# Each block of the normalised input h lies 64 bytes further on within 512 bytes than the block before it

## The chip, the cores and the metric

The kernel runs on one core of a Trainium2 chip. The metric is the device time of one execution in microseconds. Beside the times there is one profiled execution, whose trace names for each instruction its engine, its line in the kernel, its start and its duration.

## What is computed

The reference is one layer of a decoder trunk: an input of 512 positions by 1024 channels is normalised to h, h goes through one wide projection into 14,344 columns, and these feed two mixers (a chunkwise mLSTM and a differential attention), whose outputs are projected, gated, added and projected once more.

```python
h = rmsnorm(x, norm_g[l]) * (1.0 + scale[:, None]) + shift[:, None]
proj = h @ w_in[l]
(qm, km, vm, om, zm, im, fm, qa, ka, va, za, gm, ga) = jnp.split(proj, split_idx, axis=-1)
...
ym = hm @ w_proj_m[l]
...
ya = ha @ w_proj_a[l]
y = jax.nn.sigmoid(gm) * ym + jax.nn.sigmoid(ga) * ya
x = x + gate[:, None] * (y @ w_out[l])
return rmsnorm(x, final_g)
```

## The kernel before

All is float32. A product of two float32 matrices is made of three matmuls: each operand is split into a high part (`hi`, rounded to the matmul's format) and a low part (`lo`, what is left), and `mm3` (line 132) adds hi times hi, hi times lo and lo times hi into the same PSUM tile. One matmul takes 128 by 128 weights and streams up to 512 columns of the other operand, the moving one, past them. In the profile's rows the moving operand stands first behind the arrow: `acc<-h_hi,whi` is h moving over weights whi.

The normalised input lies transposed in two tiles, `h_hi` and `h_lo` (lines 338 and 339): 128 partitions, 8 blocks k of 128 channels each, 512 positions. A block is 2048 bytes of a partition. They are written block by block by ACT (line 614, high part) and DVE (line 616, low part) in the opening loop, and are read by nearly all the matmuls that follow:

- In the opening loop, block k is used in its own turn for the first columns of the attention (lines 622 to 629): six runs of three matmuls with h moving, and four with h as weights (`mm_v`).
- `proj_b` (line 342) is the projection into 128 columns, called 82 times for 656 runs: for k = 0 to 7 three matmuls of 512 columns, h moving over a weight tile (`whi`, `wlo`).
- `proj_w` (line 379) is the projection into the 512 value columns of an mLSTM head, with h as weights and the columns of `whi` and `wlo` moving: per weight tile, for four groups of positions, three matmuls with block 2q and three with block 2q + 1.
- `proj_v` (line 368), for the attention's values, is the same with 256 moving columns and twelve matmuls on a block.
- `if_gates` (line 519) has sixteen matmuls of h over one weight tile, two to a block.

`attn_proj` and `proj_m` have no h: the heads' outputs (`hh`, `hl`) move over `whi` and `wlo`. Two lines that make a sum over partitions, 509 and 510 (and 810 and 811, 837 and 838 in the mLSTM), have the constant tile `ones_r` as weights.

When the last projection of h is done, `out_weights` (line 865) reuses h's place: the output weights 0, 1 and 2 are split into blocks 0 and 1, 2 and 3, 4 and 5 of h_hi and h_lo, as 1024 elements in one piece. `out_mm` (line 974) has them moving, 512 or 256 columns at a time.

The constant tiles lie in a partition in the order in which they are named; each takes a multiple of 32 bytes. The two tiles `pad_before` and `pad_after` of 32 bytes each stand before h_hi and behind h_lo. With that, all blocks of h begin 32 bytes behind a multiple of 512. All tiles that the pools place behind them (the weights, the heads' outputs, q, k, v, the temporaries) are whole multiples of 512 bytes apart and begin at 288, that is 256 further on; the slices that the matmuls take begin at multiples of 512 bytes within them. `ones_r` lies ahead of h and begins at 224, 64 bytes before the place of the others.

TensorE takes its matmuls in the order in which the program issues them. While one matmul streams, the weights of the next are loaded.

Of the kernel before, what the change touches and what calls it, by code (L numbers as in the profile page):

```python
# [10 lines left out]
F32R = mybir.dt.float32r  # L11
# [3 lines left out]
S = 512  # L15
D = 1024
P = 128
NK = D // P
# [46 lines left out]
def hybrid_block_kernel(ctx: ExitStack, tc: tile.TileContext, xT, x, c, wada2, wada, win, wif, wpm, wpa, wout,  # L65
# [3 lines left out]
    const = ctx.enter_context(tc.tile_pool(name="const", bufs=1))  # L69
# [8 lines left out]
    def nm(s):  # L78
        _n[0] += 1
        return f"{s}_{_n[0]}"  # L80

    def tmp(w=512, dt=F32):
        return sb.tile([P, w], dt, tag="tmp", bufs=TB, name=nm("tmp"))

    def acc_ps():
        return acc.tile([P, 512], F32, tag="acc", name=nm("acc"))

    def core_ps():
        return core.tile([P, 512], F32, tag="core", name=nm("core"))
# [24 lines left out]
    def split(hi, lo, src, eng="act", scale=None):  # L114
        copy_r(eng, hi, src, scale)
        if scale is None:
            recent["dve"] = nc.vector.tensor_tensor(lo, src, hi.bitcast(F32), ALU.subtract)  # L117
        else:
            nc.vector.scalar_tensor_tensor(lo, src, scale, hi.bitcast(F32), ALU.mult, ALU.subtract)
# [5 lines left out]
    def inorder(inst):  # L125
        if last[0] is not None:
            tc.add_manual_dep(inst.ins, last[0].ins.name,
                              mybir.DependencyInfo(mybir.DependencyClass.NoSync, mybir.DependencyReason.DATA),
                              reason="issue order")
        last[0] = inst  # L130

    def mm3(ps, lhs, rhs, start, stop, head=False, swap=False):
        l, r = ((1, 0), (0, 1)) if swap else ((0, 1), (1, 0))
        a = nc.tensor.matmul(ps, lhs[0], rhs[0], start=start, stop=False)  # L134
        b = nc.tensor.matmul(ps, lhs[l[0]], rhs[l[1]], start=False, stop=False)  # L135
        c = nc.tensor.matmul(ps, lhs[r[0]], rhs[r[1]], start=False, stop=stop)  # L136
        last_mm[0] = c
        if head:
            inorder(a)
            inorder(b)  # L140
            inorder(c)

    def load_granule(src):
        raw = stg.tile([P, D], F32, tag="raw", name=nm("raw"))
        nc.sync.dma_start(raw, src)
        return raw
# [24 lines left out]
    for k in range(NK):  # L171
        t = sb.tile([P, S], F32, tag="hp", bufs=16, name=nm("xt"))
# [71 lines left out]
    for i in range(2):  # L244
        ps = core_ps()
        a = nc.tensor.matmul(ps, onesf[0:1, :], crow[:, i * S:(i + 1) * S], start=True, stop=True)
# [19 lines left out]
    for k in range(NK):  # L266
        i, start = (0, k == 0) if k < 5 else (1, k == 5)
        sq = xsum[i] if start else tmp()
        a = nc.scalar.activation(sq, xt[k], AF.Square, scale=1.0 / 32)
# [36 lines left out]
    ps = core_ps()  # L306
# [21 lines left out]
    for (a, b) in ((0, 512), (512, RL)):  # L328
        ps = core_ps()
# [5 lines left out]


    const.tile([P, 8], F32, name="pad_before")
    h_hi = const.tile([P, NK, S], F32R, name="h_hi")
    h_lo = const.tile([P, NK, S], F32R, name="h_lo")
    const.tile([P, 8], F32, name="pad_after")  # L340

    def proj_b(col, between=None):
        hi, lo = split_granule(win[GIDX[("B", col)]])
        ps = acc_ps()
        for k in range(NK):
            ksl = slice(k * P, (k + 1) * P)
            mm3(ps, (hi[:, ksl], lo[:, ksl]), (h_hi[:, k, :], h_lo[:, k, :]), k == 0, k == NK - 1)
            if k == 1 and between is not None:
                between()
        recent["pe"] = last_mm[0]  # L350
        return ps
# [68 lines left out]
    def evac_ka(ps):  # L420
        kh, kl = [], []
        for a, b in ((LO, HI), (HI, LO)):
            t, l = qk_tile(), qk_tile()
            nc.gpsimd.memset(l[b].bitcast(F32), 0.0)
            nc.scalar.copy(t[a], ps[a])
            nc.scalar.copy(t[b], ps[a])
            nc.vector.tensor_tensor(l[a], ps[a], t[a].bitcast(F32), ALU.subtract)  # L427
            kh.append(t)
            kl.append(l)
        return kh, kl  # L430
# [171 lines left out]
    for k in range(NK):  # L602
        raw = load_granule(win[GIDX[("F", k)]]) if k > 0 else first_raw
# [4 lines left out]
        a = nc.scalar.copy(hi, raw)  # L608
        issue_after(a, recent["act"])
        recent["act"] = a  # L610
        t, b = xt[k], mod[:, k:k + 1]
# [32 lines left out]
        if k == 4:  # L644
# [9 lines left out]
            a = nc.vector.tensor_scalar(agc, sm[:, SM_AG:SM_AG + 8], -0.5 / 256 * (1.0 - LAM_INIT), None, ALU.mult)  # L654
            mgc = const.tile([P, 16], F32, name="mgc")
            issue_after(a, h_dve)
            a = nc.vector.tensor_scalar(mgc, sm[:, SM_MG:SM_MG + 16], -0.25 / 4096, None, ALU.mult)
# [31 lines left out]
    for p in range(1, 4):  # L689
        for i in range(2):  # L690
# [3 lines left out]
            k = evac_ka(proj_b(C_KA + 128 * hd))  # L694
# [16 lines left out]
    ps = core_ps()  # L711
# [151 lines left out]
    wo = [None] * NK  # L863

    def out_weights(k):
        raw = stg.tile([P, D], F32, tag="raw", name=nm("raw"))
        nc.sync.dma_start(raw, wout[k])
        if k < 3:
            t = [x_[:, 2 * k:2 * k + 2, :].rearrange("p a b -> p (a b)") for x_ in (h_hi, h_lo)]
        elif k < 7:  # L870
            tag, bufs = {3: ("v", 2), 4: ("p", PB), 5: ("p", PB), 6: ("sw", 1)}[k]
            w2 = sb.tile([P, 2, D], F32R, tag=tag, bufs=bufs, name=nm("wo"))
            t = [w2[:, 0, :], w2[:, 1, :]]
        else:
            t = [stg.tile([P, D], F32R, tag=n_, name=nm(n_)) for n_ in ("whi", "wlo")]
        split(t[0], t[1], raw, eng="act")
        wo[k] = t
# [12 lines left out]
    for h in range(MH):  # L890
        q, k, v, hv = [], [], [], []
# [18 lines left out]
        for d in range(4):  # L910
            zv.append(silu2(proj_b(C_ZM + 512 * h + 128 * d)))
            tick()
            fill()
            if h == MH - 1:
                premerge(d, load_gate(d, tmp()))
                if d == 3:
                    out_weights(4)
        ssum = tmp()
        for d in range(4):
            ps = proj_b(C_OM + 512 * h + 128 * d)  # L920
            while len(hv) <= d:
                tick()
            t = tmp()
# [4 lines left out]
            else:  # L928
                t = tmp()
# [14 lines left out]
    for b in range(4, 8):  # L944
        ps = proj_b(C_GM + 128 * b, tick if b > 4 else None)
# [3 lines left out]
    for k in (3, 5, 6):  # L949
        out_weights(k)  # L950
# [4 lines left out]
    yt = []  # L955
# [12 lines left out]
    for k in (0, 1, 2, 7):  # L968
        out_weights(k)

    def rows(t):
        return slice(t * P, (t + 1) * P)

    def out_mm(ps, t, ns, ks):
        for k in ks:
            mm3(ps, (yt[k][0][:, rows(t)], yt[k][1][:, rows(t)]), (wo[k][0][:, ns], wo[k][1][:, ns]),
                k == 0, k == NK - 1)

    def residual(ps, xr, o, ns, ss):
# [8 lines left out]
    for n in range(2):  # L988
        out_mm(first[n], 0, halves[n], range(LATE))
    for t in range(NT):  # L990
        xr = stg.tile([P, D], F32, tag="raw", name=nm("xr"))
        nc.sync.dma_start(xr, x[rows(t), :])
        ss = sb.tile([P, 5], F32, tag="ss", bufs=2, name=nm("ss"))
        parts = halves if t < NT - 1 else (slice(0, 512), slice(512, 768), slice(768, D))
        os = [sb.tile([P, S], F32, tag="z", bufs=8, name=nm("o")) for _ in range(2)]
        for n, ns in enumerate(parts):
            ps = first[n] if t == 0 else acc_ps() if n % 2 == 0 else core_ps()
            ps = ps[:, 0:ns.stop - ns.start]
            out_mm(ps, t, ns, range(LATE if t == 0 else 0, NK))
            o = os[ns.start // 512][:, ns.start % 512:ns.start % 512 + ns.stop - ns.start]  # L1000
            residual(ps, xr, o, ns, ss[:, n:n + 1])
            if n < len(parts) - 1:
                nc.vector.tensor_add(ss[:, 3:4], ss[:, n:n + 1], epsc if n == 0 else ss[:, 3:4])
        n = len(parts) - 1
        nc.scalar.activation(ss[:, 4:5], ss[:, n:n + 1], AF.Sqrt, bias=ss[:, 3:4])
        nc.vector.reciprocal(ss[:, 4:5], ss[:, 4:5])
        for n, ns in enumerate(halves):
            if n == 0:
                nc.scalar.activation(os[n], xr[:, ns], AF.Copy, scale=ss[:, 4:5])
                nc.scalar.dma_start(out[rows(t), ns], os[n])  # L1010
            else:
                nc.vector.tensor_scalar(os[n], xr[:, ns], ss[:, 4:5], None, ALU.mult)
                nc.sync.dma_start(out[rows(t), ns], os[n])
# [70 lines left out]
```

## Time and profile before

| | us |
|---|---|
| median of 3 runs | 925.57 (925.35 to 926.0) |
| the profiled execution | 924.88 |
| its span, first to last instruction | 923.1 |
| TensorE, matmuls busy | 908.9 |
| VectorE (DVE) busy | 601.7 |
| ScalarE (ACT) busy | 454.9 |

The span is the part of the profiled execution's time that the trace covers. A busy time is the union of an engine's instructions. Matmuls overlap in the trace (each row lasts from its issue until its last result is through), so the pace of TensorE is the distance from one matmul's start to the next one's, which the timeline gives to 0.01 us, and not the duration in a row.

### The profile page before, as it was taken

How to read it: one execution, taken by the hardware profiler on the slowest of the kernel's cores; microseconds unless marked ns; L12 is line 12 of the kernel's file. 1: busy time of each engine (PE TensorE's matmuls, PEld its weight loads, DVE VectorE, ACT ScalarE, POOL GpSimd, SP SyncE). 2: the span in 40 equal slices, each digit the busy share in tenths (PEclk: the TensorE clock that was granted, in tenths of full speed). 3: DMA queues.
4: the chain of work that ended last, by engine and by line, in shares of the span. 5: the costliest groups of instructions: out<-in, count | busy, mean ns of one | idle time of the engine just before them, and what ended most of it. 6: DMA issues, size and time to landing. Idle time of an engine off the chain costs nothing.

```text
span 923.1 us, 11500 instructions
## 1 busy us (share of the span) xinstructions
PE 908.9 (98%) x4351; PEld 762.5 (83%) x4351; DVE 601.7 (65%) x975; ACT 454.9 (49%) x741; POOL 24.3 (3%) x56
## 2 busy tenths in 40 slices
PE   6999999999999999999999999999999999999997
PEld 3888987988888888888888888888888888888886
DVE  7967788878666565435558544586554877638944
ACT  7546887766677554222354533454233553236422
POOL 0001010000001000000000000000000000000000
PEclk8999999999999999999999999999999999999999
DMA  9863414333422352432223223223132224336421
GB/s 343 336 186 119 131 65 138 126 137 126 149 84 100 117 169 100 151 137 89 87 76 111 93 72 93 89 96 110 69 114 69 92 99 152 137 114 223 142 80 57
DMA packets 40656, 114.90 MB, mean 124 GB/s; under 512 B 8289, under 2 KB 8553, under 8 KB 39578
## 3 DMA queue, kind: packets, MB, share of 16 engines
q1 hardware_dynamic: 40010, 113.11, 35.6%
q10 hardware_dynamic: 592, 1.07, 0.4%
q8 instruction: 34, 0.56, 0.2%
q14 instruction: 20, 0.16, 0.1%
HBM read 106.78 MB, written 10.00 MB: 127 GB/s over the span
## 4 chain that ended last, share of the span: by engine, by line
PE 92%; DVE 3%; DMA 2%; ACT 2%; issue 1%; SPq 0%; ACTq 0%
PE acc L134 26%; PE acc L135 26%; PE acc L136 26%; PE core L134 3%; PE core L135 3%; PE core L136 3%; PE core L459 1%; PE core L460 1%; PE core L489 1%; DVE wlo L117 1%; DMA relt<-in_relb_dram 1%; PE core L237 1%; DMA xt<-in_xT_dram 1%; ACT whi L99 0%; DMA ga<-gt_d 0%
## 5 line engine op out<-in xcount | busy, mean ns | idle before, releaser
L134 PE MATMUL acc<-h_hi,whi 128*128 128x512 f32 x688 | 269.1, 391 | 0.5 <-DVE qk L427 0.5
L117 DVE TENSOR_TENSOR wlo<-raw,whi 128x1024 fp32r<-128x1024 f32 x129 | 157.8, 1223 | 167.7 <-ACT whi L99 163.5
L99 ACT CAST whi<-raw 128x1024 fp32r<-128x1024 f32 x129 | 135.5, 1050 | 245.5 <-PE acc L135 175.9
L135 PE MATMUL acc<-h_lo,whi 128*128 128x512 f32 x656 | 255.8, 390 | 0.0
L136 PE MATMUL acc<-h_hi,wlo 128*128 128x512 f32 x656 | 255.5, 389 | 0.0
L134 PEld LDWEIGHTS acc<-h_hi,whi 128*128 128x128 f32 x688 | 129.4, 188 | 26.6 <-PE acc L539 0.8
L136 PEld LDWEIGHTS acc<-h_hi,wlo 128*128 128x128 f32 x656 | 123.2, 188 | 25.9
L135 PEld LDWEIGHTS acc<-h_lo,whi 128*128 128x128 f32 x656 | 123.3, 188 | 23.9
L134 PE MATMUL acc<-whi,h_hi 128*128 128x512 f32 (+1 forms) x224 | 77.1, 344 | 0.1
L136 PE MATMUL acc<-whi,h_lo 128*128 128x512 f32 (+1 forms) x224 | 77.0, 344 | 0.0
L135 PE MATMUL acc<-wlo,h_hi 128*128 128x512 f32 (+1 forms) x224 | 76.9, 343 | 0.0
L134 PE MATMUL acc<-hh,whi 128*128 128x512 f32 x192 | 74.7, 389 | 0.0
L135 PE MATMUL acc<-hl,whi 128*128 128x512 f32 x192 | 74.7, 389 | 0.0
L136 PE MATMUL acc<-hh,wlo 128*128 128x512 f32 x192 | 74.7, 389 | 0.0
L134 PEld LDWEIGHTS acc<-whi,h_hi 128*128 128x128 f32 x224 | 42.4, 189 | 5.5 <-ACT tmp L741 0.5
L135 PEld LDWEIGHTS acc<-wlo,h_hi 128*128 128x128 f32 x224 | 42.4, 189 | 5.0
L136 PEld LDWEIGHTS acc<-whi,h_lo 128*128 128x128 f32 x224 | 42.4, 189 | 5.0
L464 ACT ACTIVATE pt<-pt,mn 128x128 f32<-128x128 f32 (+3 forms) x64 | 35.5, 557 | 17.6 <-DVE mn L462 17.4
L136 PEld LDWEIGHTS acc<-hh,wlo 128*128 128x128 f32 x192 | 36.1, 188 | 7.5
L135 PEld LDWEIGHTS acc<-hl,whi 128*128 128x128 f32 x192 | 36.1, 188 | 7.4
L134 PEld LDWEIGHTS acc<-hh,whi 128*128 128x128 f32 x192 | 36.1, 188 | 7.4
L462 DVE CUSTOM_DVE_ANT_0 pt<-core,bt 128x128 f32<-128x128 f32 (+3 forms) x64 | 29.5, 486 | 14.7 <-PE core L460 14.3
(277 smaller groups left out, 1360.2 us busy)
## 6 DMA issues: line engine op xcount, KB each, us to landing
raw<-in_win_dram SPq DMA_DIRECT2D x112, 512.0 KB, 3.3
wa<-in_wada_dram SPq DMA_DIRECT2D x8, 1024.0 KB, 7.1
raw<-in_wpm_dram SPq DMA_DIRECT2D x16, 512.0 KB, 3.2
raw<-in_wada_dram SPq DMA_DIRECT2D x8, 512.0 KB, 3.2
raw<-in_wpa_dram SPq DMA_DIRECT2D x8, 512.0 KB, 3.4
raw<-in_wout_dram SPq DMA_DIRECT2D x8, 512.0 KB, 3.3
gt_d<-tmp SPq DMA_DIRECT2D x12, 256.0 KB, 2.2
toe_d<-rev_d SPq DMA_DIRECT2D x8, 320.0 KB, 6.2
```

The source lines that it names most:

```text
L99: recent["act"] = nc.scalar.copy(dst, src)
L117: recent["dve"] = nc.vector.tensor_tensor(lo, src, hi.bitcast(F32), ALU.subtract)
L134: a = nc.tensor.matmul(ps, lhs[0], rhs[0], start=start, stop=False)
L135: b = nc.tensor.matmul(ps, lhs[l[0]], rhs[l[1]], start=False, stop=False)
L136: c = nc.tensor.matmul(ps, lhs[r[0]], rhs[r[1]], start=False, stop=stop)
L237: a = nc.tensor.matmul(idle, ones_r, ones_w, start=True, stop=True)
L459: inorder(nc.tensor.matmul(ps, q[m][:, qs], kh[m][:, 0:wn], start=True, stop=False))
L460: inorder(nc.tensor.matmul(ps, q[m][:, qs], kl[m][:, 0:wn], start=False, stop=True))
L462: nc.vector.tensor_tensor_reduce(pp, ps[:, 0:w], bt[:, S - w:S], 1.0, BIG, ALU.add, ALU.min, mn[:, qb, m:m + 1])
L464: nc.scalar.activation(pp, pp, AF.Exp, scale=-1.0, bias=mn[:, qb, m:m + 1], accum_out=ls[:, qb, m:m + 1])
L489: inorder(nc.tensor.transpose(ps[:, n:n + P], pt[:, 0, o:o + P], ident))
```

## The change

The two tiles get 16 more float32 elements behind each block (64 bytes), and are used as the slice without them. A block begins 2112 bytes behind the one before, which is 64 modulo 512; the eight blocks thus begin at eight different places within 512. As a piece of 1024 elements across two blocks is no longer in one piece, the output weights 0 to 2 are written with a two-block pattern and read through `wo_cols`, which turns a column range into a block and a range within it.

```diff
-    h_hi = const.tile([P, NK, S], F32R, name="h_hi")
-    h_lo = const.tile([P, NK, S], F32R, name="h_lo")
+
+    h_hi, h_lo = (const.tile([P, NK, S + 16], F32R, name=n_)[:, :, 0:S] for n_ in ("h_hi", "h_lo"))
     const.tile([P, 8], F32, name="pad_after")
...
         if k < 3:
-            t = [x_[:, 2 * k:2 * k + 2, :].rearrange("p a b -> p (a b)") for x_ in (h_hi, h_lo)]
+            t = [x_[:, 2 * k:2 * k + 2, :] for x_ in (h_hi, h_lo)]
+            raw = raw.rearrange("p (a b) -> p a b", b=S)
...
+    def wo_cols(w, k, ns):
+        if k < 3:
+            return w[:, ns.start // S, ns.start % S:ns.start % S + ns.stop - ns.start]
+        return w[:, ns]
+
     def out_mm(ps, t, ns, ks):
         for k in ks:
-            mm3(ps, (yt[k][0][:, rows(t)], yt[k][1][:, rows(t)]), (wo[k][0][:, ns], wo[k][1][:, ns]),
+            mm3(ps, (yt[k][0][:, rows(t)], yt[k][1][:, rows(t)]), [wo_cols(w_, k, ns) for w_ in wo[k]],
                 k == 0, k == NK - 1)
```

## Rows read from the trace of the kernel before

**Rows 1.** The page: span, TensorE's busy time, shares of the chain.
```profile
span 923.1 us, 11500 instructions
PE 908.9 (98%) x4351; PEld 762.5 (83%) x4351; DVE 601.7 (65%) x975; ACT 454.9 (49%) x741; POOL 24.3 (3%) x56
...
PE 92%; DVE 3%; DMA 2%; ACT 2%; issue 1%; SPq 0%; ACTq 0%
```

**Rows 2.** Stretches: us, matmuls busy (count), granted clock, DMA share, GB/s.
```profile
300.00:400.00 100.00, 99.93 (x450) 1.00 0.38 133
...
500.00:600.00 100.00, 100.00 (x462) 1.00 0.27 90
```

**Rows 3.** Groups of matmuls by form, whole span: count, busy us, mean ns, idle.
```profile
L134 PE MATMUL acc<-h_hi,whi 128*128 128x512 f32 x688 | 269.1, 391 | 0.5 <-DVE qk L427 0.5
...
L134 PE MATMUL acc<-whi,h_hi 128*128 128x512 f32 x128 | 49.9, 390 | 0.1
...
L134 PE MATMUL acc<-whi,h_hi 128*128 128x256 f32 x96 | 27.1, 283 | 0.0
...
L134 PE MATMUL core<-whi,h_hi 128*128 128x256 f32 x32 | 9.0, 282 | 0.0
...
L134 PE MATMUL core<-h_hi,whi 128*128 128x512 f32 x16 | 6.3, 396 | 0.0
...
L509 PE MATMUL core<-tmp,ones_r 128*128 128x512 f32 x8 | 3.2, 402 | 0.0
...
L810 PE MATMUL core<-tmp,ones_r 128*128 128x512 f32 x4 | 1.6, 392 | 0.0
```

**Rows 4.** Timeline of TensorE, h moving: start us, us; first and last of 69.
```profile
820.15 0.39 PE L134 MATMUL acc<-h_hi,whi 128*128 128x512 f32 x1
...
835.56 0.39 PE L136 MATMUL acc<-h_hi,wlo 128*128 128x512 f32 x1
```

**Rows 5.** Timeline of TensorE, heads' outputs moving; first and last of 20.
```profile
399.63 0.39 PE L136 MATMUL acc<-hh,wlo 128*128 128x512 f32 x1
...
403.94 0.39 PE L134 MATMUL acc<-hh,whi 128*128 128x512 f32 x1
```

**Rows 6.** Timeline of TensorE, h as weights; first and last of 11.
```profile
491.66 0.39 PE L135 MATMUL acc<-wlo,h_hi 128*128 128x512 f32 x1
...
493.93 0.39 PE L136 MATMUL acc<-whi,h_lo 128*128 128x512 f32 x1
```

**Rows 7.** Timeline of TensorE around a pair with ones_r as weights.
```profile
835.79 0.39 PE L837 MATMUL core<-tmp,ones_r 128*128 128x512 f32 x1
836.02 0.39 PE L838 MATMUL core<-tmp,ones_r 128*128 128x512 f32 x1
836.25 0.40 PE L134 MATMUL acc<-h_hi,whi 128*128 128x512 f32 x1
...
836.71 0.40 PE L136 MATMUL acc<-h_hi,wlo 128*128 128x512 f32 x1
...
837.40 0.39 PE L136 MATMUL acc<-h_hi,wlo 128*128 128x512 f32 x1
837.63 0.39 PE L134 MATMUL acc<-h_hi,whi 128*128 128x512 f32 x1
```

**Rows 8.** Timeline of TensorE, 256 columns after 512; first, second and seventh.
```profile
911.07 0.28 PE L134 MATMUL core<-h_hi,yh 128*128 128x256 f32 x1
911.18 0.28 PE L135 MATMUL core<-h_lo,yh 128*128 128x256 f32 x1
...
911.78 0.28 PE L134 MATMUL core<-h_hi,yh 128*128 128x256 f32 x1
```

**Rows 9.** Timelines of ACT, DVE and TensorE: the last output weights kept in h.
```profile
863.99 1.05 ACT L99 CAST h_hi<-raw 128x1024 fp32r<-128x1024 f32 x1 [1.44 <-DMA raw<-in_wout_dram]
871.29 1.22 DVE L117 TENSOR_TENSOR h_lo<-raw,h_hi 128x1024 fp32r<-128x1024 f32 x1
874.58 0.39 PE L135 MATMUL acc<-h_lo,yh 128*128 128x512 f32 x1
```

## The prediction, made blind

> **What bounds the kernel now.** I read the page's busy shares and the shares of the chain first: TensorE is busy for 908.9 of 923.1 us, and 92% of the chain that ended last is its matmuls [rows 1]. The table by stretches of 100 us says that this holds all along: of the eight from 100 to 900 us, two of which stand in [rows 2], each is covered by matmuls at 99.4% or more, at a granted clock of 1.00, which is the 2.4 GHz level. There is no wait to be removed. The time is a sum over matmuls of the distance from one start to the next, so I went to the timeline of TensorE for that distance. The duration in the groups [rows 3], 389 ns, is not it: matmuls overlap.
>
> With h as moving operand, 68 distances from 820.15 to 835.56 us make 15.41 us: 226.6 ns each [rows 4]. 512 columns at 2.4 GHz are 213.3 ns, so each matmul has 13.3 ns on top. The change moves addresses only, so the question is whether these 13.3 ns, or their evenness, depend on addresses.
>
> By the placement told with the kernel, the trace holds three alignments (start of the moving operand less start of the weights, modulo 512): 256 where h moves over weights [rows 4], 0 where the heads' outputs move [rows 5], and 256 with the parts swapped where h is the weights [rows 6]. The distances are 226.6, 4.31 us / 19 = 226.8 and 2.27 us / 10 = 227 ns: the same. From this alone alignment would be no matter, or one of 256 would be none.
>
> One operand stands elsewhere: ones_r, as weights, lies 64 bytes before the place of all others. Its two matmuls come in the middle of a run of 512-column ones with no change of width and no idle time [rows 7]. From 835.56, where [rows 4] end, to 837.63 there are nine distances and 2.07 us; nine even ones are 2.040. So about 0.03 us are lost (0.02 to 0.04, since rows are given to 0.01), and the matmul durations of 0.40 between show where; the groups of these pairs have 392 and 402 ns in place of 389 to 391 [rows 3]. The first two distances, in which ones_r's weights are loaded, make 0.46 in place of 0.453: 7 ns. The six from 836.02 to 837.40, after the return to the usual place, make 1.38 in place of 1.360: 20 ns. There are 16 such pairs in the kernel (lines 509, 810 and 837); 13 of them lie between 512-column matmuls, and these 13 all behave so. This is the row nearest to the change, and it says that a step of 64 bytes between one matmul and the next is not free, and that the even distance comes back only after some five or six matmuls.
>
> **The change part by part.** *Placement.* Block k of h starts 64k bytes further on within 512, h_hi and h_lo alike. Each of the two tiles grows by 8 x 64 = 512 bytes, so all that lies behind moves by 512 or 1024: nothing else changes its alignment. No instruction, wait or DMA is added or taken away, and no queue's order is edited.
>
> *h as moving operand.* There are 688 + 16 = 704 runs of three matmuls on one block [rows 3]. The 656 of the single-column projections step to the next block at each run; in the opening loop one block serves all the runs of its turn, so some 16 steps are left there, and 8 in the gates' projection: 680 steps, each forward by 64 for the moving operand (the way from block 7 back to block 0 is -448, the same as +64). Weights 64 bytes back and a moving operand 64 bytes on are the same change of the distance between the two, so a step is the first part of [rows 7]: 7 ns. 680 x 7 ns = 4.8 us. Ends: nothing below is excluded by a reason. The gain nearest by is the first 256-column matmul after 512-column ones: its distance is 0.11 us where the five that follow make 0.60, 0.12 each, so some 10 ns are saved once at a change of rhythm [rows 8]; with rows given to 0.01 that is no other size than the 7 ns, and 680 x -7 ns = -4.8 us. Above, each step could cost what the return costs, 20 ns: 13.6 us. I take 7 because direction and size are those of the row; the 20 stands for the other direction.
>
> *h as weights.* In the wide projection (128 runs of three, from the 128-count group of [rows 3]) the block alternates between two neighbours, forward and back. Two steps are then one pair like ones_r's, 27 ns: 128 / 2 x 27 ns = 1.7 us. Ends: -128 x 7 = -0.9 and 128 x 20 = 2.6 us. In the 256-column projections (96 in the group of [rows 3], and 32 more in the opening loop) four runs share a block, so there are some 32 steps; the weights step forward, which is the return's direction: 32 x 20 ns = 0.6 us, at least -0.2.
>
> *The output weights kept in h.* wo 0 to 2 are now cut at 512 columns. ACT and DVE still write 1024 elements with one instruction each, 1.05 and 1.22 us; the last of them ends at 872.51 and is first read by the matmul at 874.58 [rows 9]: 2.07 us cover it, and even a DVE instruction of twice its length would add only 1.22, so I put it at nothing; without that cover it would be those 1.22. As moving operands these blocks step some 20 times in the output projection: 20 x 7 ns = 0.1 us.
>
> *What hides, and what is late next.* Nothing hides a longer distance on TensorE, for it has no idle time; DVE and ACT, which wait for it, only wait longer. Equally, nothing else is late when TensorE is.
>
> *Sum.* 4.8 + 1.7 + 0.6 + 0.1 = 7.2 us. The profiled execution took 924.88 us (span 923.1), and by its own terms becomes 932.1. The median of the runs is 925.57, 0.69 higher, and as the terms are counts of matmuls they come on top of either: 932.1 to 932.8. I give 932.1.
>
> **A rule weighed against the rows.** [Rows 4 to 6] show one distance at alignments 0 and 256, [rows 7] an uneven one at a step of 64. The Trainium skill (SBUF — State Buffer, "Who interferes with whom") gives TensorE two read ports of its own, one for the moving operand and one for weights, independent of each other, and says that it never waits on anyone. By that rule the change is worth nothing; the trace agrees at 0 and 256 and disagrees at ones_r.
>
> **The rivals.**
> *No dependence.* By this the change does nothing that TensorE can see. Then ones_r's unevenness is of something else: its matmuls read a tile that DVE has just written, in another queue of work, and the same unevenness follows a change from 256 to 512 columns, where no address steps. For it: equal distances in [rows 4 to 6]. Against it: other matmuls that wait for DVE or ACT in the middle of a run lose nothing. Time: 924.9 by the profiled execution, 925.6 by the median.
>
> *Each step saves.* If weights and moving operand meet in memory and the 13.3 ns are that meeting, a moving operand that starts 64 bytes further on may slip past it, as the first 256-column matmul after wide ones does with 0.11 in place of 0.12 [rows 8]. 680 x -7 = -4.8 us, the alternating weights and the rest about 0: 920.1. If instead one half of the 13.3 ns went at all 2112 matmuls with h moving, three to each of the 704 runs, it would be 2112 x 6.7 = 14 us, 911. For it: 13.3 ns stand there to be had. Against it: no stretch of the trace, at any alignment, has 512-column matmuls steadily closer than 226.6. The Trainium skill (TensorE: Matmul & The Clock Gate, "Wait — 56ns, not 53.3ns?") gives 215.7 ns for 512 columns back to back; an estimate from it is 2112 x 10.9 ns = 23 us less, and no row here shows such a distance.
>
> *Each step costs its most.* Every step, in either direction, pays the 20 ns of the return: 13.6 + 2.6 + 0.6 = 16.8 us, 942. It decides from the point at which the even distance is regained within three matmuls, so that each step pays in full; [rows 7] shows it regained only after six, which speaks against the full price.
>
> **How the numbers follow.** A step costs, by 7 to 13 ns (932 to 937): 0.44. A step costs its most: 0.04. No dependence: 0.21. Each step saves: 0.31, of it 0.08 for the larger saving. The likeliest is the first, and its time is 932.1; its own range is 928 to 938. A measurement of this kernel can tell about 0.2% (1.85 us) from no change. Faster by more than that: 0.31; within: 0.21; slower: 0.48. The range has to take in the saving of the steps (920.1) and most of the costly side: 918 to 940. It leaves out the larger saving and the full price, some 0.12 to 0.15.
>
> **What would show each step.** In the stretch at 820 us the 68 distances with h moving give 226.6 ns before; by my forecast they give about 229, with matmul durations of 389 to 396 mixed by block, while the matmuls over the heads' outputs at 400 us stay at 227. A mean of 389 ns in all groups and the same distance show the second case; distances under 226 the third. The wide projection at 491 us should go from 227 to about 231. DVE's and ACT's durations for wo should be as before. The prediction is wrong if the unevenness is not that of a step in address, or if direction is of no matter; a difference in the first 23 us, where TensorE waits, would be none of this.

## The result, and the profile after

The changed kernel takes 935.93 us (median of 3 runs, 934.03 to 936.26) against 925.57: a ratio of 1.0111, 95% interval 1.0097 to 1.0124, that is 10.4 us more. The profiled executions agree: 935.93 us with a span of 934.1, against 924.88 and 923.1, 11.0 us more. The likeliest case of the forecast, 932.1 us within 928 to 938, had the direction and about two thirds of the size (7.2 us).

The page of the kernel after, as in [rows 1]: span, busy engines, shares of the chain.

```profile
span 934.1 us, 11500 instructions
PE 921.4 (99%) x4351; PEld 762.3 (82%) x4351; DVE 602.2 (64%) x975; ACT 454.9 (49%) x741; POOL 24.8 (3%) x56
...
PE 94%; DVE 2%; DMA 2%; ACT 1%; issue 0%; SPq 0%
```

The counts are the same, DVE and ACT are as busy as before, and TensorE's busy time has grown by 12.5 us. The order of the instructions on TensorE is the same too. So the 11 us are longer distances between the same matmuls. The groups by form, which answer to [rows 3] (mean duration in ns behind the bar), already say whose; the first line is of before, for a group that [rows 3] do not show, and the second block is of after:

```profile
L135 PE MATMUL acc<-h_lo,whi 128*128 128x512 f32 x656 | 255.8, 390 | 0.0
```
```profile
L134 PE MATMUL acc<-h_hi,whi 128*128 128x512 f32 x688 | 271.7, 395 | 0.3 <-DVE qk L427 0.3
L135 PE MATMUL acc<-h_lo,whi 128*128 128x512 f32 x656 | 259.9, 396 | 0.0
...
L134 PE MATMUL acc<-hh,whi 128*128 128x512 f32 x192 | 74.9, 390 | 0.0
...
L134 PE MATMUL acc<-whi,h_hi 128*128 128x512 f32 x128 | 50.4, 395 | 0.0
...
L134 PE MATMUL acc<-whi,h_hi 128*128 128x256 f32 x96 | 27.0, 282 | 0.0
```

391, 390 and 390 ns have become 395, 396 and 395 where h takes part in a 512-column matmul of the projections; the heads' outputs (`hh`) are at 390, and the 256-column ones have gone from 283 to 282. The timeline of TensorE shows the pace: h moving, in the stretch of [rows 4]; h as weights, as in [rows 6]; and the heads' outputs, as in [rows 5].

```profile
831.10 0.40 PE L135 MATMUL acc<-h_lo,whi 128*128 128x512 f32 x1
...
833.88 0.40 PE L135 MATMUL acc<-h_lo,whi 128*128 128x512 f32 x1
...
836.66 0.40 PE L135 MATMUL acc<-h_lo,whi 128*128 128x512 f32 x1
```
```profile
344.50 0.40 PE L134 MATMUL acc<-whi,h_hi 128*128 128x512 f32 x1
...
347.28 0.40 PE L134 MATMUL acc<-whi,h_hi 128*128 128x512 f32 x1
```
```profile
398.80 0.39 PE L134 MATMUL acc<-hh,whi 128*128 128x512 f32 x1
...
403.56 0.39 PE L134 MATMUL acc<-hh,whi 128*128 128x512 f32 x1
```

Between each two of the first three rows lie twelve distances, four blocks of h: 2.78 us, 231.7 ns each, where it was 226.6. The two halves take the same time, as they would if the pattern repeated after four blocks, that is after 256 bytes. The second stretch has 2.78 us / 12 = 231.7 ns (227 before), the third 4.76 / 21 = 226.7: as before.

Summed from each start to the next over the whole span, the same matmuls in both kernels, the difference lies as follows.

| matmuls | count | before, us | more after, us |
|---|---|---|---|
| h moving over weight tiles, 512 columns (tile `acc`) | 2062 | 470.8 | 9.0 |
| h as weights, 512 columns moving | 384 | 87.5 | 1.7 |
| h as weights, 256 columns moving | 384 | 46.0 | -0.5 |
| output projection | 216 | 43.7 | 0.3 |
| heads' outputs moving | 576 | 130.6 | 0.2 |
| the first 22 us | 28 | 17.8 | 0.4 |

That sums to 11.1 us; the 701 matmuls that are not in the table (scores, sums over partitions, the gates and some of the opening's) differ by less than 0.1 together. What the prediction rested on is in the first two rows; the question for the experiments is why.

### The profile page after: what moved, and what is told of

It reads as the page before. It is cut to its first block, busy times and chain, and to the rows that moved or that the text cites. A ratio compares the mean times of both kernels' runs of the same rounds, so it can differ in the third digit from the quotient of the medians.

```text
span 934.1 us, 11500 instructions
## 1 busy us (share of the span) xinstructions
PE 921.4 (99%) x4351; PEld 762.3 (82%) x4351; DVE 602.2 (64%) x975; ACT 454.9 (49%) x741; POOL 24.8 (3%) x56
## 4 chain that ended last, share of the span: by engine, by line
PE 94%; DVE 2%; DMA 2%; ACT 1%; issue 0%; SPq 0%
PE acc L135 26%; PE acc L134 26%; PE acc L136 26%; PE core L135 4%; PE core L136 4%; PE core L134 4%; PE core L459 1%; PE core L460 1%; PE core L489 1%; DMA relt<-in_relb_dram 1%; DMA xt<-in_xT_dram 1%; PE core L237 1%; DVE wlo L117 1%; DMA raw<-in_win_dram 0%; PE core L330 0%
## 5 line engine op out<-in xcount | busy, mean ns | idle before, releaser
L135 PE MATMUL acc<-h_lo,whi 128*128 128x512 f32 x656 | 259.9, 396 | 0.0
L136 PE MATMUL acc<-h_hi,wlo 128*128 128x512 f32 x656 | 258.3, 394 | 0.0
```

## The experiments

The theory on record is that a *step* costs: TensorE loses time when the distance in address between the moving operand and the weights changes from one matmul to the next, and regains its even pace only after some six. Its rival in what follows is that the *place* costs: a distance other than 0 (modulo 256) is slow by itself, with no step. All kernels below have the instructions of the kernel before, in its order on TensorE, and only place tiles elsewhere. "Distance" is always the start of the moving operand less that of the weights, modulo 256; in the kernel before it is 0 for all but the constant tiles (ones_r and the identity among them).

### A constant 64

```diff
-    const.tile([P, 8], F32, name="pad_before")
+    const.tile([P, 24], F32, name="pad_before")
...
-    const.tile([P, 8], F32, name="pad_after")
+    const.tile([P, 120], F32, name="pad_after")
```

> All blocks of h lie 64 bytes further on than before, without any step between them; nothing else changes its place. Step theory (what costs is a change of the distance between moving operand and weights from one matmul to the next): no time beside before, 925.6 us, within 1 us, and 226.7 ns from matmul to matmul in the stretch at 820 us. Place theory (a place other than 0 or 256 away from the weights costs by itself, 4 to 5 ns per matmul): some 2062 x 4.5 ns = 9 us with h moving and 1.7 with h as weights, 936 us.

Measured: 934.09 us against 925.14, ratio 1.0095 (1.0080 to 1.0110). There is no step between blocks in this kernel, and it costs nearly all that the change costs. In the timeline the pace is even, and slow:

```profile
827.66 0.40 PE L134 MATMUL acc<-h_hi,whi 128*128 128x512 f32 x1
...
831.16 0.40 PE L134 MATMUL acc<-h_hi,whi 128*128 128x512 f32 x1
```

Fifteen distances, 3.50 us: 233.3 ns, and so for the whole stretch. Not a transient that dies out, but 6.7 ns on every matmul. Only 38 of the 82 single-column projections settle there; the other 44 settle near 229 ns, at the same distance of 64. One of them follows 15 us later:

```profile
845.62 0.39 PE L134 MATMUL acc<-h_hi,whi 128*128 128x512 f32 x1
...
849.05 0.39 PE L134 MATMUL acc<-h_hi,whi 128*128 128x512 f32 x1
```

Fifteen distances in 3.43 us are 228.7 ns. So the 2062 matmuls lose 7.3 us (3.5 ns each), those with h as weights 2.3. What decides between the two levels is open. The step theory in the form of the prediction is refuted here: a step is not needed.

### A step of 256

```diff
+H_OFF = [0, 2112, 512, 2624, 1024, 3136, 1536, 3648]
...
-    h_hi = const.tile([P, NK, S], F32R, name="h_hi")
-    h_lo = const.tile([P, NK, S], F32R, name="h_lo")
+    class Blocks:
+        def __init__(self, name):
+            self.t = const.tile([P, H_SIZE], F32R, name=name)
+
+        def __getitem__(self, at):
+            _, k, sl = at
+            return self.t[:, H_OFF[k] + (sl.start or 0):H_OFF[k] + (S if sl.stop is None else sl.stop)]
...
```

> Odd blocks of h lie 256 bytes further on than even ones: a step at each block as in the changed kernel, but of 256 bytes. Step theory with a period of 256 bytes: 925.6 us, within 1 us. Step theory with a period of 512 or more, or any step at all: 672 steps at 13.4 ns and 128 at 13.4 ns, 936 us. Place theory: 925.6 us, since both places occur in the kernel before at the same distance from start to start.

Measured: 925.63 us against 925.14, ratio 1.0006 (0.9997 to 1.0016): no difference. Its group of h moving (line 137 in this kernel) has the mean of [rows 3]:

```profile
L137 PE MATMUL acc<-h_hi,whi 128*128 128x512 f32 x688 | 269.0, 391 | 0.4 <-DVE qk L440 0.4
```

A step at every block that keeps the place modulo 256 is free. It also clears part of the rest of the change: larger tiles and blocks that are not one behind the other cost nothing. The output weights, which the change splits at 512 columns, stay in one piece here.

### Other constant places

```diff
-    const.tile([P, 8], F32, name="pad_before")
+    const.tile([P, 40], F32, name="pad_before")
...
-    const.tile([P, 8], F32, name="pad_after")
+    const.tile([P, 104], F32, name="pad_after")
```

This is the one for 128; the others for 192 and 32 differ in the two sizes, and for 16 the blocks begin 4 elements into their tile.

> All blocks of h 128 bytes further on than before, no steps. After the constant 64 cost a whole 6.7 ns per matmul in its quiet stretches (233.3 for 226.7 ns), the step theory has fallen and the place theory stands. By it this kernel shows the level of the distance 128: if every distance other than 0 (modulo 256) costs the same, 233.3 ns in quiet stretches and 934 us, as with 64. If the cost grows with the distance, 240 ns and 943. If a meeting of the two reads is what costs and is gone halfway, 220 ns or less and 912 us.

> All blocks of h 192 bytes further on (64 back, modulo 256), no steps. Place theory: the level of the distance 192. With the constant 64, h as weights stood at 192 from the moving operand and had 233.3 ns; so 233.3 ns with h moving, 934 us. With h as weights the distance is 64 here. Step theory: 925.6, as it has been for the constant 64, which was wrong there.

> All blocks of h 32 bytes further on, no steps: half of the smallest shift tried. If the distance counts in pieces of 64 bytes, either as before (226.7 ns, 925.6 us) or as with 64 (233.3 ns, 934 us). If it counts in finer pieces, between the two: 230 ns, 930 us.

> All blocks of h 16 bytes further on, no steps. If any distance other than a multiple of 256 costs: 233.3 ns in quiet stretches and 935 to 939 us as with 32, 64, 128 and 192. If the distance counts in pieces of 32 bytes or more and 16 falls into the piece of 0: 226.7 ns and 925.6 us. If a small distance lets one read run just ahead of the other, under 226.7 ns and under 920 us: the version that would beat both.

| h further on by | us | ratio (interval) | h moving, ns more per matmul over the span |
|---|---|---|---|
| 16 | 934.11 | 1.0102 (1.0088 to 1.0116) | 4.1 |
| 32 | 939.03 | 1.0149 (1.0132 to 1.0167) | 5.7 |
| 64 | 934.09 | 1.0095 (1.0080 to 1.0110) | 3.5 |
| 128 | 938.84 | 1.0144 (1.0126 to 1.0163) | 5.1 |
| 192 | 939.21 | 1.0155 (1.0138 to 1.0171) | 5.8 |

Quiet stretches, h moving, at 192, at 128 and at 16 (line 137 there):

```profile
831.35 0.40 PE L134 MATMUL acc<-h_hi,whi 128*128 128x512 f32 x1
...
834.85 0.39 PE L134 MATMUL acc<-h_hi,whi 128*128 128x512 f32 x1
```
```profile
831.21 0.39 PE L134 MATMUL acc<-h_hi,whi 128*128 128x512 f32 x1
...
834.69 0.39 PE L134 MATMUL acc<-h_hi,whi 128*128 128x512 f32 x1
```
```profile
831.55 0.40 PE L137 MATMUL acc<-h_hi,whi 128*128 128x512 f32 x1
...
834.33 0.40 PE L137 MATMUL acc<-h_hi,whi 128*128 128x512 f32 x1
```

Fifteen distances in 3.50 us (233.3 ns), fifteen in 3.48 (232.0) and twelve in 2.78 (231.7). With h moving, every place tried other than a multiple of 256 is slow; none is faster than 226.7 ns, not even 16 bytes away. The cost doesn't grow with the distance (128 and 192 are alike, and 32 is as dear), so neither of the two sharper versions expected of the constant 128 holds. The 939 us where 934 were expected are h moving too: at 32 and 192 nearly all single-column projections run at 233 ns, where 44 of those of the constant 64 run at 229.

With h as weights there is an exception, in the kernel with h 16 bytes further on (the distance is 240 then): the first of the four wide projections is slow and the other three are not.

```profile
344.68 0.40 PE L137 MATMUL acc<-whi,h_hi 128*128 128x512 f32 x1
...
348.18 0.40 PE L137 MATMUL acc<-whi,h_hi 128*128 128x512 f32 x1
```
```profile
493.20 0.39 PE L138 MATMUL acc<-wlo,h_hi 128*128 128x512 f32 x1
...
496.60 0.39 PE L138 MATMUL acc<-wlo,h_hi 128*128 128x512 f32 x1
```

Fifteen distances each, 3.50 us (233.3 ns) and 3.40 (226.7). One distance can thus settle at the slow pace or at the fast one, as the constant 64 settles at two paces. The distance doesn't decide alone; at a distance of 0, no undisturbed stretch looked at here settled at anything but 226.7 ns.

### All tiles moved together

```diff
-    const.tile([P, 8], F32, name="pad_before")
+    const.tile([P, 24], F32, name="pad_before")
```

> h and all that lies behind it (weights, heads' outputs, q, k, v, temporaries) 64 bytes further on: distances between moving operands and weights are those of the kernel before, but every one of them stands at another place within 256. If only the distance between moving operand and weights matters: 925.6 us, within 1.5 (ones_r alone stays and is now 128 away, some 0.5 us). If each operand's own place within 256 is what matters: all 512-column matmuls pay 6.7 ns, 3400 of them, some 20 us: 945 us.

Measured: 925.47 us against 925.14, ratio 1.0003 (0.9993 to 1.0013). So what costs hangs on the distance between the operands, and not on where either of them stands. The trace of this kernel has the counterpart in it: h moving is at 391 as before, and the pairs with ones_r, which did not move along and are now 128 away, have become slower, 404 ns where [rows 3] have 392.

```profile
L134 PE MATMUL acc<-h_hi,whi 128*128 128x512 f32 x688 | 269.2, 391 | 0.5 <-DVE qk L427 0.5
...
L810 PE MATMUL core<-tmp,ones_r 128*128 128x512 f32 x4 | 1.6, 404 | 0.0
```

### The weights step along

```diff
-        hi = stg.tile([P, D], F32R, tag="whi", name=nm("whi"))
-        lo = stg.tile([P, D], F32R, tag="wlo", name=nm("wlo"))
+        hi = stg.tile([P, D + 128], F32R, tag="whi", name=nm("whi"))
+        lo = stg.tile([P, D + 128], F32R, tag="wlo", name=nm("wlo"))
+        if step:
+            hi, lo = (t.rearrange("p (k n) -> p k n", n=P + 16)[:, :, 0:P] for t in (hi, lo))
+            raw = raw.rearrange("p (k n) -> p k n", n=P)
...
-        hi, lo = split_granule(win[GIDX[("B", col)]])
+        hi, lo = split_granule(win[GIDX[("B", col)]], step=True)
...
-            mm3(ps, (hi[:, ksl], lo[:, ksl]), (h_hi[:, k, :], h_lo[:, k, :]), k == 0, k == NK - 1)
+            mm3(ps, (hi[:, k, :], lo[:, k, :]), (h_hi[:, k, :], h_lo[:, k, :]), k == 0, k == NK - 1)
```

> The changed kernel, and in the 82 single-column projections the eight blocks of the weight tiles step by 64 bytes too, so that moving operand and weights keep their distance while both step. If the distance between the two is what matters: the 9.0 us with h moving go, the 1.7 with h as weights stay, 927 to 928 us. If the moving operand's own step is what matters (with no regard to the weights): 936 us as in the changed kernel. If it is the step of the weights alone, or each step for itself: more than 936.

Measured: 935.18 us against 925.14, ratio 1.0108 (1.0092 to 1.0125): next to nothing is won back, and the first expectation fails. The profiled execution took 931.82 us, less than the other three, because its opening is 3.5 us shorter than that of the changed kernel; behind the opening, the two spans differ by 0.6 us. The timeline (h moving, 24 distances in 5.56 us) has 231.7 ns, just as the changed kernel:

```profile
826.04 0.40 PE L134 MATMUL acc<-h_hi,whi 128*128 128x512 f32 x1
...
831.60 0.40 PE L134 MATMUL acc<-h_hi,whi 128*128 128x512 f32 x1
```

In this kernel each matmul is at distance 0 from the weights that it *uses*. But the weights that are *loaded while it streams* are those of the next matmul, and in one matmul of three they belong to the next block, 64 bytes on. If the distance that counts is that to the weights being loaded, one matmul of three is at 192, and the other two must regain their pace each time, which the next experiment shows they don't. That the distance to the weights in use alone is what counts, is refuted. The reading with the weights being loaded fits but has no kernel of its own, since in all the others the two distances go together. The second expectation, that the moving operand's own step costs whatever the weights do (936 us), fits the time as well; by the constant 64 it can't be the whole cost, but no run here separates it from the reading with the weights being loaded.

### Place and step together: alternating blocks, and halves

The first with odd blocks 64 bytes further on than even ones, the second with blocks 4 to 7 further on than 0 to 3 (`Blocks` as above).

```diff
+H_OFF = [0, 2064, 512, 2576, 1024, 3088, 1536, 3600]
```
```diff
+H_OFF = [0, 512, 1024, 1536, 2064, 2576, 3088, 3600]
```

> Odd blocks of h 64 bytes further on than even ones: as many steps as in the changed kernel, half of the matmuls at distance 0 and half at 64. If the time is the sum of what each distance costs when it is constant: half of the 7.3 us that the constant 64 cost with h moving, half of its 2.3 us with h as weights, some 0.5 us elsewhere: 5.3 us, 930.5. If a matmul at distance 0 also loses where it follows one at 64 (as blocks 0 and 4 of the changed kernel do, 230.5 for 227.5 ns), 1031 x 3 ns = 3.1 us more: 933.5 us. If the steps cost 13.4 ns each and the place nothing: 936 us.

> Blocks 0 to 3 as before, blocks 4 to 7 all 64 bytes further on: two steps in 24 matmuls in place of eight, and none between the two blocks of a wide weight tile. Step theory: 82 x 2 steps, each at least the 13.4 ns of the changed kernel and up to 27 since eleven matmuls follow in which the even distance can be regained: 2.2 to 4.4 us more than before, 928 to 930 us. Place theory: half of the matmuls with h moving at 4.5 ns, 4.6 us, and half of those with h as weights, 0.9 us: 931 us.

Measured: alternating 938.10 us, ratio 1.0143 (1.0129 to 1.0157); halves 932.23 us, ratio 1.0071 (1.0056 to 1.0086). Both are above every time expected of them (936 and 931 us at most). Both have the same number of matmuls at 0 and at 64. By the constant 64, half of the matmuls with h moving would lose 3.6 us; with two steps in 24 matmuls they lose 4.6, with eight 10.0, which is more than in the constant 64 itself. The timeline of the alternating kernel (line 137, the first matmul of a block; even, odd, even, and so on):

```profile
830.62 0.40 PE L137 MATMUL acc<-h_hi,whi 128*128 128x512 f32 x1
...
831.31 0.40 PE L137 MATMUL acc<-h_hi,whi 128*128 128x512 f32 x1
...
832.01 0.40 PE L137 MATMUL acc<-h_hi,whi 128*128 128x512 f32 x1
...
832.71 0.40 PE L137 MATMUL acc<-h_hi,whi 128*128 128x512 f32 x1
```

Blocks at 0 and at 64 alike take 0.69 or 0.70 us for three matmuls, where three at an even 226.7 ns take 0.68. So steps do matter, on top of the place: a block at distance 0 is only fast if the ones before it were. That half of the prediction's mechanism stands. The place alone doesn't give the 10.0 either.

The halves show a step in each direction by itself (line 137 again; block 0 after block 7, then block 4 and block 5, then block 0 of the next projection):

```profile
829.71 0.40 PE L137 MATMUL acc<-h_hi,whi 128*128 128x512 f32 x1
...
832.48 0.40 PE L137 MATMUL acc<-h_hi,whi 128*128 128x512 f32 x1
...
833.18 0.39 PE L137 MATMUL acc<-h_hi,whi 128*128 128x512 f32 x1
...
835.24 0.40 PE L137 MATMUL acc<-h_hi,whi 128*128 128x512 f32 x1
```

On the way back from 64 to 0, twelve distances make 2.77 us where even ones make 2.72: 0.05 us, and the even pace comes back only at the last two or three of the twelve. On the way on to 64, the first three make 0.70 us and the next nine 2.06, 228.9 ns each: 0.01 to 0.02 us above the pace that this half settles at.

### The constant tiles at the others' place

```diff
+    const.tile([P, 16], F32, name="pad_const")
     ident = const.tile([P, P], F32, name="ident")
...
-    const.tile([P, 8], F32, name="pad_before")
+    const.tile([P, 120], F32, name="pad_before")
```

> The kernel before with its three constant tiles (the identity, the ones and ones_r) 64 bytes further on, so that they too stand at a multiple of 256 from all others. If the distance explains the pairs with ones_r as weights, their 0.03 us go: nine distances from the matmul ahead of such a pair make 2.04 in place of 2.07 us, durations 389 in place of 392 to 402 ns, and 13 pairs give 0.4 us, which a measurement does not tell from 925.1. If the pairs have their unevenness from something else, it stays.

Measured: 924.23 us against 925.12, ratio 0.9994 (0.9985 to 1.0003): no difference that can be told, as expected. The trace is what this kernel was for (the same pair as in [rows 7], one line lower in this kernel):

```profile
834.50 0.39 PE L136 MATMUL acc<-h_hi,wlo 128*128 128x512 f32 x1
834.73 0.39 PE L838 MATMUL core<-tmp,ones_r 128*128 128x512 f32 x1
834.96 0.39 PE L839 MATMUL core<-tmp,ones_r 128*128 128x512 f32 x1
...
836.54 0.39 PE L134 MATMUL acc<-h_hi,whi 128*128 128x512 f32 x1
```

Nine distances, 2.04 us, where it was 2.07; no 0.40 is left between them, and so in all 13 pairs that lie between 512-column matmuls. The unevenness of these pairs is that of the distance in address, and of nothing else: the data, the waits and the queue are the same here. The 402 ns of line 509 in [rows 3] are not of the distance, for they stay (one line lower):

```profile
L510 PE MATMUL core<-tmp,ones_r 128*128 128x512 f32 x8 | 3.2, 402 | 0.0
```

Three of these eight come behind a narrower matmul, one of them with a wait.

### A version under both

The prediction had noted that a 256-column matmul can come closer [rows 8], and the table of the result shows the 256-column ones gaining. In the constant 64 their duration fell to 279 ns. This kernel is the last one with the weight tiles of the attention's values, which move over h there, 192 bytes further on:

```diff
-    def split_granule(src):
+    def split_granule(src, off=0):
...
-        hi, lo = split_granule(win[GIDX[("A", col, half)]])
+        hi, lo = split_granule(win[GIDX[("A", col, half)]], 48)
```

> The kernel before with the constant tiles at a multiple of 256 from all others, and with the weight tiles of the attention's values (256 columns moving over h) 192 bytes further on within 256. In the constant 64, where these matmuls had the same distance of 192, the 384 of them took 44.6 us in place of 46.0, 3.5 ns less each, while all 512-column ones got slower. If narrow matmuls gain at this distance also when the wide ones keep theirs, 288 x 3.5 ns = 1.0 us go, and 0.2 to 0.4 of the constant tiles: 923.9 us, 0.13% under 925.1. If the gain there was paid by the matmuls around them, the time is that of the constant tiles alone, 924.2 to 925.1 us.

Measured: 923.34 us against 925.05, ratio 0.9986 (0.9975 to 0.9997). It has the lowest median of all here, 0.14% under the kernel before, with an interval that ends just under 1. The moved constant tiles are part of that (924.23 us by themselves), and the times alone don't separate the two. The timeline has the gain at its place, the 42 distances of a run:

```profile
99.31 0.28 PE L134 MATMUL acc<-whi,h_hi 128*128 128x256 f32 x1
...
104.26 0.28 PE L134 MATMUL acc<-whi,h_hi 128*128 128x256 f32 x1
```

4.95 us / 42 = 117.9 ns. In the kernel before the same projection has 36 distances in 4.32 us, 120 ns each:

```profile
99.55 0.28 PE L134 MATMUL acc<-whi,h_hi 128*128 128x256 f32 x1
...
103.87 0.28 PE L134 MATMUL acc<-whi,h_hi 128*128 128x256 f32 x1
```

Over the span all 256-column matmuls with h as weights take 1.2 us less, and nothing else pays for it.

## Why the prediction came out as it did

- *The bound.* Right: TensorE's distances are the time, and nothing hid the longer ones. The sum over them, 11.1 us, is the difference of the spans, 11.0, to 0.1.
- *The reading of the three alignments.* "One of 256 would be none" was the right half of that sentence, and "alignment would be no matter" the wrong one. The step of 256 and the tiles moved together show both.
- *The reading of ones_r.* Right that its 0.03 us are of the 64 bytes: they go when it is moved. Wrong that they are the price of a *step* alone. The step that failed is "the even distance comes back only after some five or six matmuls": it came back there because the operands were at distance 0 again. In the constant 64, where they never are, it doesn't come back at all. The 402 ns of line 509 were no evidence of the distance.
- *h moving, 680 x 7 ns = 4.8 us.* Too small by nearly half: 9.0 us, 13.2 ns for each step. The term was sized by two distances of one pair, 0.46 us for 0.453, and a difference of 7 ns lies within the rounding of rows given to 0.01 us. In the nanoseconds of the trace these two distances lose 2 ns in every one of the 13 pairs, and the six that follow lose 25 where all six are of 512 columns: the pair had nearly its whole cost on the return. The upper end of the case, 13 ns, would have given 8.8. Both directions are in the halves: there too the way back costs more (0.05 us) than the way on (0.01 to 0.02), but it is also the way to another place, and no kernel with blocks 64 bytes *back* each time was run, so whether direction by itself matters stays open.
- *h as weights, 1.7 us.* Measured 1.7. The size is right; but the reason given, two steps that make a pair, is not shown to be the cause, as the constant 64 makes 2.3 without steps.
- *256 columns, +0.6 us.* Wrong in sign: -0.5. The price of 512-column matmuls was put on 256-column ones. [Rows 8] pointed the other way and were kept for the rival alone.
- *The output weights kept in h.* Right: the last DVE instruction still takes 1.21 us and ends at 881.92, well ahead of the matmul that needs it at 885.29; 0.3 us are lost in the matmuls of the output projection, 0.1 was forecast.
- *Not in the sum.* The heads' outputs and the opening lose 0.6 us together, the former probably in the first matmuls behind a projection of h, which was not tried apart.
- *The rule weighed.* By the Trainium skill (SBUF — State Buffer, "Who interferes with whom") the two reads of TensorE are independent and it waits on no one. Here the pace depends on the distance between its two operands, 226.7 ns at 0 and up to 233.3 elsewhere, while both standing elsewhere together costs nothing; the measurement decides, for this kernel's float32 matmuls with new weights each time.
- *The rivals.* "No dependence" is refuted by the five constant places. "Each step saves" is refuted for 512 columns by the kernels with steps, the changed one, the alternating one and the halves, which are all slower. 256-column matmuls do gain, but by the place 192 and without a step, in a kernel of its own.
- *Its own signs.* The stretch at 820 us was to go to about 229 ns and went to 231.7; the heads' outputs at 227 and the wide projection at about 231 came as said (226.7 and 231.7). The prediction was to be wrong if the unevenness is not that of a step in address. It is that of a distance in address, to which a step adds.
- *Luck.* That the time came out near the forecast owes something to chance. By the same mechanism the constant 64, which has no step between blocks, would have stayed at 925.6 us, and it takes 934.09, nearly what the changed kernel takes.

Still open is how place and step combine. If each block of the changed kernel paid what its distance costs when constant (0, 3.5, 5.1 and 5.8 ns in turn, 3.6 in the mean), the 2062 matmuls would lose 7.4 us; they lose 9.0. The alternating kernel loses 10.0 for 3.6. A rule that gives all of these numbers was not found, nor what lets one distance settle at two paces.

## What to carry to other kernels

Where TensorE is the bound and every matmul brings new weights, compare the pace of matmuls of one shape with different operands: 226.7 against 233.3 ns is 3% and shows in no wait and no idle time. Keep moving operands and weights of 512-column matmuls at the same place modulo 256 bytes, blocks as well as tiles, and look at what a small tile in front of them does to it. And a single odd operand in the trace of before can show what a change of layout will do, but its price has to be taken from where it stays, not from where it passes by.

## What the runs showed that was not expected

A shift of 16 bytes between moving operand and weights is enough to cost 4.1 ns on each of 2062 matmuls. In quiet stretches the constant places settle near 232 or at 233.3 ns against 226.7, and two projections of one kernel can settle at different paces: at 229 and at 233 in the constant 64, and with h as weights at 233.3 and at 226.7 in the kernel with 16 bytes. And the same distance that slows a 512-column matmul speeds up a 256-column one, 117.9 for 120 ns.
